# Queueing the modulation products behind the last traced VectorE instruction

## The chip, the cores and the metric

The kernel runs on one core of a Trainium2 chip. The metric is the device time of one execution in microseconds. The program is written in a tile language: a trace of instructions is written out in Python, and a scheduler then fixes the order of each engine's queue at build time, by data dependences, buffers and priorities. On the chip each queue is worked off in that order. The engines are TensorE (PE; its weight loads are PEld), VectorE (DVE), ScalarE (ACT), GpSimd (POOL), and SyncE (SP), which issues the DMAs.

## The reference

Two layers of a diffusion backbone on 256 latent tokens and 256 context tokens, 1024 features wide. A layer is: half-step SwiGLU feed-forward, three token mixers side by side, half-step SwiGLU feed-forward. Each of them is modulated by nine vectors per stream that come from a conditioning vector:

```python
sc, scc = silu(c), silu(c_ctx)
mx = (sc @ w_ada[i] + b_ada[i]).reshape(bsz, N_MOD, 1, D_MODEL)     # latent
mc = (scc @ w_ada[i] + b_ada[i]).reshape(N_MOD, D_MODEL)            # context
def half_ffn(h, g_pre, g_post, shift, scale, gate, w1, w2):
    return 0.5 * gate * rms_norm(swiglu(modulate(rms_norm(h, g_pre), shift, scale), w1, w2), g_post)
```

`w_ada` is 1024 x 9216 per layer: a matrix times two vectors, and large to load. The feed-forward has 2816 hidden features. Shift, scale and gate of the first feed-forward are modulations 0 to 2, of the mixers 3 to 5, of the second feed-forward 6 to 8.

## The kernel before

Activations lie with features on the 128 partitions and 512 tokens (context, then latent) along the columns. To keep float32 accuracy in the fast matmul format, every weight tile and every activation tile is split into a high and a low half. `wload` loads a 512 KB tile `raw` (3 buffers), ScalarE rounds it to `whi`, VectorE subtracts to get `wlo` (2 buffers each). `gemm` then runs three matmuls per tile: weight high with activation high and low, weight low with activation high.

`ffn(l, half)` works in three slabs of hidden features (8, 7 and 7 tiles of 128). A **hidden step** `hidden(k)` projects one pair of tiles: 48 matmuls, then SiLU on ScalarE, the product `gV` on VectorE (line 96), `B` high on ScalarE and `B` low on VectorE (line 102). After a slab's hidden steps come eight **output steps**, which multiply the slab by the output weights and add to `y` (line 99; in slab 0 ScalarE copies). In slab 0 the first `early` steps (4, 5 or 6) run on one 256-column segment at a time, in which norm work of the stage before (`rest`) is woven in; slab 2 also runs one segment after the other; all the rest runs on 512 columns.

The modulation vectors are not matmuls: `ada_block` (line 269) takes one 512 KB tile of `w_ada` (`araw`, 2 buffers, loaded by `ada_fetch` on SP's queue, one block ahead), and multiplies its two halves by the broadcast SiLU of each condition, with a sum along the columns: four VectorE products of 128x512 per block (two where the context is no longer needed, from modulation 5 of layer 1 on), each followed by a read of the accumulator (line 288). After each eighth block small additions finish one vector.

`tick(share)` hands these blocks out in the feed-forward: `due` is the number of blocks that the stage owes (48 in `ffn(0,0)`, 40 in `ffn(0,1)`, 40 in `ffn(1,0)`), and each step earns a share of it: 2 of `whole` after a 512-column hidden step beyond `early`, 1 after an output step of slabs 0 and 1 and after a hidden step of slab 2's first segment, half of one after that segment's output steps. `whole` is 49, 47 and 45. A block is traced under `high_priority(offset=-100)`: the scheduler treats it as if it stood 100 instructions later, so that it fills gaps. That priority is all that orders it against the feed-forward work. The trace is scheduled as a whole, so a block whose tile has landed can also be issued long before the place where it was traced. `cols` (line 372) reads finished vectors and traces at once what is still missing of them (`need`). In layer 0, `vectors()` queues the loads of constants on SP's queue behind the last load of `w_ada`.

Of the kernel before, what the change touches and what calls it, by code (L numbers as in the profile page):

```python
# [58 lines left out]
class Net:  # L59
# [238 lines left out]
    def tick(self, share):  # L298

        self.credit += share * self.due  # L300
        while self.credit > 0.999 and self.todo:
            self.credit -= 1
            with self.tc.high_priority(offset=-100):
                self.ada_block(*self.todo.pop(0))

    def need(self, l, j):
# [1255 lines left out]
```

## Time and profile before

| | us |
|---|---|
| median of 3 runs | 2545.29 |
| lowest and highest | 2538.87, 2552.49 |
| the profiled execution's own time | 2550.41 |
| its span, first to last instruction | 2548.6 |
| PE busy | 2425.2 |
| DVE busy | 1819.8 |
| ACT busy | 1159.9 |
| POOL busy | 289.1 |

The mean granted clock of TensorE is 0.977 of full speed. Busy time of PE includes time at the slow clock, and pipelined matmuls overlap, so a busy PE is not PE at its peak. Products of line 288 by the ticks run from 84 to 284 us, from about 1110 to 1310 and from about 1505 to 1653. The stages can be told by their steps: in `ffn(0,0)` the hidden steps of slab 0 end at 155 us, of slab 1 at 286, and slab 2 runs from 325 to 446, with the first segment's hidden steps up to 363 and its output steps up to 382. In `ffn(0,1)` the first segment of slab 2 runs from 1360 to 1419, in `ffn(1,0)` from 1738 to 1796.

### The profile page before, as it was taken

To read this page: it belongs to the slowest core of one execution; us is meant where nothing else is said; L and a number is where in the kernel's file an instruction comes from. 1 tells how busy PE (TensorE), PEld (TensorE's weight loads), DVE (VectorE), ACT (ScalarE), POOL (GpSimd) and SP (SyncE) were. 2 spreads that over 40 slices of the span, in tenths; PEclk is the share of its full clock that TensorE was granted. 3 is DMA by queue.
4 is the path that set the end of the run, shared out by engine and by line. 5 is a ranking of instruction groups with operands and counts; after the bars stand their busy time and mean duration, and the time that the engine had idled before them with its cause. 6 is when DMAs were issued, how large, how long until landed. Compare 5 with 4: busy or idle time off the path is not lost. (4 is left out here: it accounts for less than half of the span.)

```text
span 2548.6 us, 40627 instructions
## 1 busy us (share of the span) xinstructions
PE 2425.2 (95%) x15554; PEld 2119.7 (83%) x15554; DVE 1819.8 (71%) x3820; ACT 1159.9 (46%) x1935; POOL 289.1 (11%) x288
## 2 busy tenths in 40 slices
PE   6999999999999999989999999999999889998998
PEld 4878799777788767888789998889978779887997
DVE  5898658899875564588864798635789977675555
ACT  3422246656443443563323563224566534455443
POOL 1000002202100111230000230000221110011001
PEclk8999999999999999989999999999999889998999
DMA  6676456443212412556754558735554332433654
GB/s 236 206 223 217 154 176 205 142 149 104 88 53 72 132 53 80 187 164 229 239 167 154 181 184 267 256 100 161 179 174 149 88 101 86 165 127 122 190 185 138
DMA packets 150796, 400.58 MB, mean 157 GB/s; under 512 B 39621, under 2 KB 50629, under 8 KB 150601
## 3 DMA queue, kind: packets, MB, share of 16 engines
q1 hardware_dynamic: 150600, 397.99, 49.4%
q8 instruction: 122, 2.00, 0.3%
q14 instruction: 74, 0.60, 0.1%
HBM read 382.72 MB, written 15.20 MB: 156 GB/s over the span
## 5 line engine op out<-in xcount | busy, mean ns | idle before, releaser
L114 PE MATMUL mm<-B,whi 128*128 128x256 f32 (+1 forms) x7632 | 1325.6, 322 | 35.0 <-ACT B L93 18.0
L114 PEld LDWEIGHTS mm<-B,whi 128*128 128x128 f32 x7632 | 1116.7, 190 | 156.8 <-ACT B L93 21.5
L93 ACT ACTIVATE whi<-raw 128x1024 fp32r<-128x1024 f32 (+1 forms) x506 | 524.6, 1037 | 583.4 <-PE mm L114 537.0
L102 DVE TENSOR_TENSOR wlo<-raw,whi 128x1024 fp32r<-128x1024 f32 (+1 forms) x506 | 613.8, 1214 | 169.9 <-ACT whi L93 141.5
L114 PE MATMUL mm<-B,wlo 128*128 128x256 f32 (+1 forms) x3816 | 692.6, 320 | 10.1 <-DVE wlo L102 10.0
L114 PEld LDWEIGHTS mm<-B,wlo 128*128 128x128 f32 x3816 | 565.6, 188 | 67.5 <-DVE wlo L102 13.9
L114 PE MATMUL mm<-B,araw 128*128 128x512 f32 (+1 forms) x1104 | 224.9, 351 | 4.7 <-DVE araw L102 4.2
L114 PEld LDWEIGHTS mm<-B,araw 128*128 128x128 f32 x1104 | 176.8, 191 | 31.9 <-DVE araw L102 5.6
L288 DVE SCALAR_TENSOR_TENSOR araw<-araw,P 128x512 f32<-128x512 f32 x256 | 167.8, 685 | 28.2 <-DMA araw<-in_w_ada 28.1
L93 ACT ACTIVATE B<-gV 128x256 fp32r<-128x256 f32 (+1 forms) x124 | 58.1, 468 | 241.7 <-DVE gV L96 241.5
L99 POOL TENSOR_TENSOR gm<-gm,ge 128x256 f32<-128x256 f32 x33 | 33.9, 1027 | 1110.0 <-ACT ge L93 1106.0
L288 DVE SCALAR_TENSOR_TENSOR gx<-araw,P 128x512 f32<-128x512 f32 x192 | 125.8, 687 | 41.9 <-DMA araw<-in_w_ada 41.6
L96 DVE TENSOR_TENSOR gV<-gS,mm 128x256 f32<-128x256 f32 (+1 forms) x124 | 59.7, 481 | 108.3 <-PE mm L114 93.4
L99 DVE TENSOR_TENSOR P<-P,mm 128x256 f32<-128x256 f32 (+1 forms) x88 | 43.2, 491 | 103.9 <-PE mm L114 103.9
L105 DVE SCALAR_TENSOR_TENSOR cv<-xp,vec,cv 128x512 f32<-128x512 f32 (+1 forms) x160 | 111.4, 704 | 2.1 <-ACT cv L93 1.4
L93 ACT ACTIVATE gS<-mm 128x256 f32<-128x256 f32 (+1 forms) x172 | 75.4, 439 | 33.9 <-PE mm L114 31.8
L102 DVE TENSOR_TENSOR araw<-raw,araw 128x1024 fp32r<-128x1024 f32 x56 | 70.0, 1250 | 27.2 <-PE mm L114 13.7
L93 ACT ACTIVATE araw<-raw 128x1024 fp32r<-128x1024 f32 x56 | 59.3, 1059 | 60.3 <-PE mm L114 43.0
L99 POOL TENSOR_TENSOR P<-P,gV 128x512 f32<-128x512 f32 (+1 forms) x30 | 36.1, 1203 | 238.9 <-DVE gV L105 235.4
L102 DVE TENSOR_TENSOR B<-gV,B 128x256 fp32r<-128x256 f32 (+1 forms) x124 | 62.4, 503 | 0.0
L93 ACT ACTIVATE B<-gR,mod 128x256 fp32r<-128x256 f32 x88 | 43.3, 501 | 34.7 <-DVE gR L105 25.8
L102 POOL TENSOR_TENSOR B<-gK,B 128x256 fp32r<-128x256 f32 x44 | 43.9, 998 | 111.5 <-ACT gK L93 111.5
(269 smaller groups left out, 2206.6 us busy)
## 6 DMA issues: line engine op xcount, KB each, us to landing
raw<-in_w_ffn_in SPq DMA_DIRECT2D x248, 512.0 KB, 4.1
raw<-in_w_in SPq DMA_DIRECT2D x144, 512.0 KB, 3.6
araw<-in_w_ada SPq DMA_DIRECT2D x130, 512.0 KB, 4.4
raw<-in_w_ffn_out SPq DMA_DIRECT2D x88, 448.0 KB, 3.3
raw<-in_w_ffn_out SPq DMA_DIRECT2D x32, 512.0 KB, 4.5
raw<-in_w_branch SPq DMA_DIRECT2D x24, 512.0 KB, 3.6
raw<-in_w_out SPq DMA_DIRECT2D x24, 512.0 KB, 3.6
P<-keep SPq DMA_DIRECT2D x20, 256.0 KB, 5.9
```

The lines of the kernel that those rows point to most:

```text
L93: self.nc.scalar.activation(out=out, in_=in_, func=func, **kw)
L96: (eng or self.nc.vector).tensor_tensor(out, a, b, op=ALU.mult)
L99: (eng or self.nc.vector).tensor_tensor(out, a, b, op=ALU.add)
L102: (eng or self.nc.vector).tensor_tensor(out, a, b, op=ALU.subtract)
L105: self.nc.vector.scalar_tensor_tensor(out, a, s, b, op0=op0, op1=op1)
L114: self.nc.tensor.matmul(out, lhsT=lhsT, rhs=rhs, start=start, stop=stop)
L288: self.nc.vector.scalar_tensor_tensor(o, wh, 1.0, self.cond[s][h], op0=ALU.mult, op1=ALU.mult, accum_out=c)
```

## The change

In `tick`, the last VectorE instruction traced so far is looked up, and the block is traced under `issue_after` of it: each VectorE instruction of the block gets an edge for the order of issue, behind that instruction on VectorE's queue. It is an edge of order alone, with no wait for a result. The block's DMA on SP is not on VectorE and gets no edge. Blocks traced by `need` are not touched.

```diff
         while self.credit > 0.999 and self.todo:
             self.credit -= 1
-            with self.tc.high_priority(offset=-100):
+            after = next(i for i in reversed(self.nc.cur_bb.bb.instructions) if i.engine == mybir.EngineType.DVE)
+            with self.tc.high_priority(offset=-100), self.tc.issue_after(after):
                 self.ada_block(*self.todo.pop(0))
```

## Rows read from the trace of the kernel before

**Rows 1.** The page's busy times: us, share of the span, instructions.
```profile
PE 2425.2 (95%) x15554; PEld 2119.7 (83%) x15554; DVE 1819.8 (71%) x3820; ACT 1159.9 (46%) x1935; POOL 289.1 (11%) x288
```

**Rows 2.** PE's waits, 80:340 and 1105:1345 (total, times, longest); busy by engine, 1500:1660.
```profile
PE mm L114 <- ACT B L93: 8.2, 2, 4.4
PE mm L114 <- DVE wlo L102: 2.8, 4, 1.0
PE mm L114 <- DVE B L102: 0.6, 1, 0.6
...
PE mm L114 <- ACT B L93: 2.4, 1, 2.4
...
1500.00:1660.00 160.00, 157.40 (x892) 137.16 (x892) 126.88 (x295) 61.06 (x88) 6.30 (x5) 1.00 0.78 253
```

**Rows 3.** Slices of 10 us: PE, PEld, DVE, ACT, POOL busy; PE clock; DMA share, GB/s.
```profile
150.00:160.00 10.00, 5.00 (x15) 3.47 (x15) 9.76 (x32) 2.17 (x3) 0.00 (x0) 0.83 0.65 211
...
170.00:180.00 10.00, 10.00 (x45) 8.23 (x44) 9.06 (x25) 3.03 (x4) 0.00 (x0) 1.00 0.72 226
...
280.00:290.00 10.00, 6.06 (x18) 4.12 (x17) 7.58 (x21) 1.58 (x2) 0.00 (x0) 0.79 0.50 169
290.00:300.00 10.00, 10.00 (x40) 8.07 (x40) 1.74 (x3) 1.91 (x2) 0.00 (x0) 0.87 0.29 93
```

**Rows 4.** Timeline, slab 0's end in `ffn(0,0)`: start, us, what, [idle before, releaser].
```profile
149.83 1.31 PE L114 MATMUL mm<-B,wlo 128*128 128x512 f32 x5
...
154.18 0.68 DVE L96 TENSOR_TENSOR gV<-gS,mm 128x512 f32<-128x512 f32 x1
...
155.58 0.51 PE L114 MATMUL mm<-B,whi 128*128 128x512 f32 x1 [4.44 <-ACT B L93]
```

**Rows 5.** Instructions of line 288 alone: one hidden step, then `ffn(0,0)` from 80.
```profile
142.40:154.20 11.80, 7.58 (x26) 1.00 0.75 236
...
80.00:340.00 260.00, 122.50 (x384) 0.98 0.63 200
```

**Rows 6.** DVE's timeline: two hidden multiplies with no products between.
```profile
1676.00 0.69 DVE L96 TENSOR_TENSOR gV<-gS,mm 128x512 f32<-128x512 f32 x1 [4.28 <-PE mm L114]
...
1686.99 0.69 DVE L96 TENSOR_TENSOR gV<-gS,mm 128x512 f32<-128x512 f32 x1 [4.28 <-PE mm L114]
```

**Rows 7.** Columns of rows 3: slab 2's first segments (hidden, output), then early steps of `ffn(1,0)`.
```profile
325.00:363.00 38.00, 38.00 (x338) 38.00 (x336) 21.46 (x28) 19.47 (x28) 0.00 (x0) 1.00 0.58 184
363.00:382.00 19.00, 19.00 (x164) 19.00 (x163) 12.23 (x20) 10.58 (x16) 3.09 (x3) 1.00 0.64 189
...
1360.00:1399.00 39.00, 39.00 (x333) 39.00 (x332) 20.97 (x28) 19.09 (x27) 0.00 (x0) 1.00 0.58 179
1399.00:1419.00 20.00, 20.00 (x172) 20.00 (x171) 13.17 (x22) 11.28 (x17) 3.15 (x3) 1.00 0.60 187
...
1506.00:1549.00 43.00, 43.00 (x366) 42.94 (x366) 41.81 (x88) 24.47 (x42) 5.59 (x4) 1.00 0.74 237
```

**Rows 8.** Line 288, whole span: what DVE sat idle for (us, times).
```profile
  DMA araw<-in_w_ada: 69.7, 69
```

**Rows 9.** Tile `masks`: first reader (duration ns min/median/max, first and last start).
```profile
L114 PE MATMUL ps<-gV,masks x8: 275/275/310, 493.8 to 1907.8; 128*128 128x48 f32 x8
```

**Rows 10.** Timelines beside and after GpSimd work; GpSimd's group in slab 2's first segment.
```profile
1108.61 1.69 POOL L99 TENSOR_TENSOR gAV<-gAV,ge 128x256 f32<-128x256 f32 x1 [1.46 <-ACT ge L93]
1109.62 0.96 DVE L102 TENSOR_TENSOR B<-gV,B 128x256 fp32r<-128x256 f32 x1
...
1116.68 0.41 DVE L102 TENSOR_TENSOR B<-gV,B 128x256 fp32r<-128x256 f32 x1
...
L99 POOL TENSOR_TENSOR gm<-gm,ge 128x256 f32<-128x256 f32 x3 | 3.1, 1029 | 300.9 <-ACT ge L93 300.9
```

**Rows 11.** SP's queue, 80:340: waits of `ada_fetch` for its buffer (total, times, longest).
```profile
SPq L266 <- DVE araw L288: 70.0, 40, 3.1
```

## The prediction

> **What bounds the kernel now.** I read the busy shares first. TensorE (PE) is busy 95% of 2548.6 us [rows 1], so an edit that only reorders VectorE (DVE) work can win back no more than PE's idle time and its slow-clock time, and only in the stretches that the edit touches. The products of `ada_block` (line 288) are issued by ticks in three feed-forward stages: `ffn(0,0)`, `ffn(0,1)` and `ffn(1,0)`. So the second view is PE's waits in those three stretches [rows 2]. In the first, PE waits 8.2 us in two waits for ScalarE's high half of a hidden tile (`B`), 2.8 us for a weight low half and 0.6 us for a hidden low half: 11.6 us. In the second, one such wait of 2.4 us. In the third PE idles 160.0 - 157.4 = 2.6 us in all.
>
> The reader is to see in [rows 3] what such a wait costs beyond itself. At the full clock 10 us hold 45 matmuls. The slice 150 to 160 has 5.00 us of PE time but only 15 matmuls (22.5 would fit), at a granted clock of 0.83; 280 to 290 has 18 in 6.06 us (27 would fit), at 0.79; 290 to 300 has 40. The missing 7.5, 9 and 5 at 10/45 = 0.22 us are 4.8 us lost to the lower of the clock's two levels after the two long waits. In the other two stretches the clock stays at 1.00.
>
> Who is late? [rows 4] shows the chain at the end of the first slab. PE has its last matmul of hidden step 7 done at 149.83 + 1.31 = 151.14. The DVE multiply that makes the hidden tile (`gV`, line 96) runs only at 154.18, and PE resumes at 155.58, through ScalarE. In between DVE was working off products: between two such multiplies (142.4 to 154.2) there are 26 instructions of line 288, that is 13 products, each with its accumulator read [rows 5]. The ticks trace less than that: 48 blocks over 49 shares, two shares a step, are 1.96 blocks, and at four products a block 7.8 products a step. So products traced after this step's multiply already stand in front of it. They were free to: nothing but their own data tied them to a place. An undisturbed 512-column step takes 10.99 us [rows 6]; the disturbed one took 11.8.
>
> **The change part by part.** No computation or DMA is added or removed. Each block's DVE instructions must be issued behind the last DVE instruction traced before its tick: after a hidden step that is the low half of that step's own tile (or a later step of the woven norm work), in an output step the weight's low half or the accumulation.
>
> *The slab ends.* The step of [rows 5] had 11.8 us of DVE, of which 13 products at 122.50/192 = 0.64 us are 8.3 us; 3.5 us are other work. With eight products it is 8 x 0.64 + 3.5 = 8.6 us against PE's 10.99, so the multiply is no longer late: five products fewer are 3.2 us, against a lateness of 3.04. Gone then, at most: 11.6 + 4.8 + 2.4 + 2.6 = 21.4 us. At least: if order within the step still leaves the multiplies half as late, about 11. I take 21.4, since eight products leave 2.4 us spare.
>
> *The waits for the products' own weights.* DVE stood 69.7 us in 69 waits at the head of its queue for `araw` to land [rows 8]. With two buffers and at most two blocks a step these loads get a step's time, and much of this goes. I count it at nothing by itself: what it cost PE is in the 21.4.
>
> *Where the products go.* They can no longer run ahead, so the last ones land in slab 2's first segment, where today there is none. For `ffn(0,0)` that is 7 hidden steps of 0.98 block and 8 output steps of 0.49, or 10.8 blocks of 4 x 0.64 = 2.55 us: 27.5 us of DVE. The segment has 38 + 19 = 57 us, PE has no gap in it, and DVE is busy 21.5 + 12.2 us [rows 7]. The sum is 61.2, so 4.2 us too much. For `ffn(0,1)` (40 blocks over 47 shares) it is 9.4 blocks or 23.9 us, on 21.0 + 13.2, which makes 58.1 of 59 us: full. For `ffn(1,0)` (40 over 45) it is 9.8 blocks, by then of two products each, 12.5 us: room enough. Cover: the blocks are traced with a priority 100 instructions later than their place, so overflow can slip into the second segment. Low end of this cost: 0 (below nothing is excluded, PE has no idle time there). High end: the 4.2 us fall on PE, and both full segments end with a wait like the 4.44 us of [rows 4] and its 1.7 us of slow clock: 4.2 + 12.3 = 16.5 us. I take 4, nearer the low end, because a row carries a like load: 1506 to 1549 of `ffn(1,0)`, also 256-column steps, has 41.8 of 43 us of DVE, 237 GB/s, and PE busy throughout [rows 7].
>
> *What moves with it on SP's queue.* The loads of `araw` follow their buffers, about 90 us later at the end of `ffn(0,0)`; the constants that `vectors()` queues behind the last of them (masks, rotary tables) come as much later. The masks are first read at 493.8 us [rows 9] and the last tick's block runs near 385, so nothing is late. `cols` asks for modulation 4 at the end of slab 1, when 37 of 48 blocks are traced and 24 are needed.
>
> *A rule against it.* Beside a GpSimd operation the 128x256 low half took 0.96 us, without one 0.41 [rows 10]. The Trainium skill ("SBUF — State Buffer", section "Who interferes with whom") says that a VectorE instruction with two SBUF inputs and a GpSimd instruction that reads SBUF exclude one another for a whole instruction. The trace agrees in kind. Products have two SBUF inputs and would now stand beside GpSimd's three sums of squares in each segment [rows 10]. By the rule in full, 3 x 1.03 us in each of the two full segments, the cost would be 6.2 us and the forecast 2 us later. By the row it is 3 x 0.55 us in each, 3.3 us, which lies inside the 4.
>
> **Sum.** 21.4 - 4 = 17.4 us off the profiled execution's 2550.4, which gives 2533. The runs' median, 2545.3, is 5.1 lower, and the same difference gives 2528. The runs span 13.7 us (0.54%), so half a per cent (12.7 us) is about what can be told from no change.
>
> **The rivals.**
> *Slab 2 takes it back.* The cost is its high end, 16.5: net 5, 2540. For it: DVE at 61.2 of 57 us. Against: the second segment and the priority as cover. Chance 0.22.
> *Slower: SP's queue becomes the bound.* A load of `araw` waits on SP for its buffer, with the weight loads queued behind it: 70.0 us in 40 waits, 1.75 each [rows 11]. In 512-column steps a weight tile is due every 5.3 us (24 matmuls at 0.22) and hides that; in slab 2 every 2.7 us (24 at 38/338). If DVE lags and the 10.8 + 9.4 + 9.8 = 30 loads that move there each pass the wait on to PE: 52.5 us, less 21.4, so +31 and 2576. It decides once the wait exceeds what the third `raw` buffer covers (about one tile, 2.7 us; the longest wait so far is 3.1). Against: 1506 to 1549 loads at 237 GB/s in such steps without a PE gap. Chance 0.12.
> *The change does little.* The scheduler already placed most blocks behind their step, or other late work keeps the waits: 2545. Against: 13 products where 7.8 are traced, and none at all in slab 2. Chance 0.12.
> The forecast, 2528 with a range of its own from 2519 to 2539: chance 0.54.
>
> **How the numbers follow.** Faster by over 0.5% is below 2532.6: about 0.7 of the forecast's chance and a fifth of the first rival's, 0.42. Slower by over 0.5% is above 2558: the second rival and little else, 0.13. The rest, 0.45, is within. The range reaches down to 2514 (no cost in slab 2, and a run at the low end of the spread) and up to 2556 (both mild rivals with the spread); it leaves out the slower rival.
>
> **What would show it.** Right: no wait of PE over 1 us at the ends of slabs 0 and 1 of `ffn(0,0)`, no slice below 0.95 there, seven to nine products between two hidden multiplies, none before the fifth hidden step, products in the slab 2 segments until about 385 us, and the 69.7 us of DVE waits for `araw` below 30. Wrong: new PE waits for `wlo` or `B` in slab 2, or SP's waits for `araw` above 2.7 us there.

## The result and the profile after

The changed kernel takes 2512.1 us (median of 5 runs, 2511.01 to 2519.57), the kernel before 2544.3 (5 runs on the same chip, 2538.87 to 2552.49). The ratio is 0.9878, with a 95% interval of 0.9864 to 0.9893: 32 us faster by the medians. Measured a second time, on another occasion (`c_after_again` below), it was 2517.16 against 2544.13, ratio 0.9891 (0.9867 to 0.9916): 27 us. The forecast of 2528 was too high: the first median lies 1.9 us under the range (2514 to 2556), the second inside it.

The busy times of the changed kernel answer to [rows 1]. Its span is 2509.2 us, its mean granted clock 0.984 where it was 0.977.

```profile
PE 2404.5 (96%) x15554; PEld 2107.3 (84%) x15554; DVE 1819.5 (73%) x3820; ACT 1165.7 (46%) x1935; POOL 289.7 (12%) x288
```

PE lost 20.7 us of busy time with the same 15,554 matmuls; DVE's busy time is as it was. So part of what went was no wait but matmuls at the lower clock.

PE runs its matmuls in the same order in every kernel of this study, but for at most 190 of 15,554 places (4 between before and after). The stages can therefore be cut at matmuls of the same number, and compared one by one, without regard to when they run. All times are us from one profiled execution each, PE's idle time in brackets where there was any that matters.

| stage | before | before again | after | after again |
|---|---|---|---|---|
| `ffn(0,0)`, slabs 0 and 1 after the early steps | 221.4 (11.8) | 219.4 (11.7) | 202.9 (0.0) | 202.9 (0.0) |
| its slab 2 | 119.5 | 119.5 | 119.7 | 120.9 (1.0) |
| mixers, layer 0 | 595.7 | 597.9 | 594.5 | 596.4 |
| `ffn(0,1)`, slabs 0 and 1 | 197.4 (4.6) | 199.1 (4.8) | 191.9 (0.0) | 191.9 (0.0) |
| its slab 2 | 126.7 | 126.7 | 126.4 (0.7) | 127.5 (0.3) |
| `ffn(1,0)`, slabs 0 and 1 | 184.8 (2.6) | 186.2 (2.8) | 181.1 (0.0) | 181.1 (0.0) |
| its slab 2 | 121.0 | 121.0 | 119.5 | 121.0 |
| mixers, layer 1 | 446.8 | 442.5 | 438.5 | 439.5 |

By the means of two traces each, slabs 0 and 1 of the three stages gained 17.5 + 6.3 + 4.4 = 28.2 us, and the three slabs 2 together lost 0.3 (367.2 before; 365.6 and 369.4 after). That is 27.9 us, and it lies between the two measured differences. Layer 1's mixers, where no tick hands out a product, are 5.7 us shorter by the same means; what is known of that stands in the last section.

The reader is to see first that the stalls and their aftermath are gone. These are the 10-us slices that answer to [rows 3], with the same columns: 45 or 46 matmuls in each, at full clock.

```profile
150.00:160.00 10.00, 10.00 (x46) 8.19 (x45) 9.27 (x29) 3.21 (x4) 0.00 (x0) 1.00 0.66 222
...
170.00:180.00 10.00, 10.00 (x45) 8.19 (x45) 9.49 (x27) 3.32 (x4) 0.00 (x0) 1.00 0.82 252
...
280.00:290.00 10.00, 10.00 (x45) 8.20 (x44) 9.26 (x27) 2.08 (x3) 0.00 (x0) 1.00 0.74 236
290.00:300.00 10.00, 10.00 (x45) 8.22 (x44) 9.73 (x28) 2.02 (x2) 0.00 (x0) 1.00 0.71 224
```

The timelines of DVE and of PE at the end of slab 0 answer to [rows 4]. The multiply `gV` now waits for PE (2.53 us idle before it), it no longer keeps PE waiting: it starts at 145.62, and PE goes from the weight low half of one tile to the next without a bracket of idle time.

```profile
145.62 0.69 DVE L96 TENSOR_TENSOR gV<-gS,mm 128x512 f32<-128x512 f32 x1 [2.53 <-PE mm L114]
146.22 1.22 DVE L102 TENSOR_TENSOR wlo<-raw,whi 128x1024 fp32r<-128x1024 f32 x1
147.36 0.68 DVE L102 TENSOR_TENSOR B<-gV,B 128x512 fp32r<-128x512 f32 x1
147.96 0.69 DVE L288 SCALAR_TENSOR_TENSOR gx<-araw,P 128x512 f32<-128x512 f32 x1
```

```profile
148.55 1.77 PE L114 MATMUL mm<-B,wlo 128*128 128x512 f32 x7
150.15 0.62 PE L114 MATMUL mm<-B,whi 128*128 128x512 f32 x2
150.61 0.39 PE L114 MATMUL mm<-B,wlo 128*128 128x512 f32 x1
150.84 2.45 PE L114 MATMUL mm<-B,whi 128*128 128x512 f32 x10
```

Line 288 alone, in the hidden step before that, answers to [rows 5]: 16 instructions, eight products, where the prediction counted 13. Below it is what DVE sat idle for on that line in the whole run, against 69.7 us in [rows 8].

```profile
134.60:145.60 11.00, 5.06 (x16) 1.00 0.59 193
```

```profile
  DMA araw<-in_w_ada: 6.1, 12
```

The first segment of slab 2 answers to [rows 7]: hidden steps, output steps, and then the beginning of the second segment, all engines. After it, the same three stretches with line 288 alone on DVE.

```profile
304.00:342.00 38.00, 38.00 (x334) 37.88 (x333) 37.30 (x86) 18.43 (x27) 0.00 (x0) 1.00 0.86 274
342.00:361.00 19.00, 19.00 (x162) 18.82 (x162) 19.00 (x43) 9.90 (x15) 2.02 (x2) 1.00 0.82 269
361.00:400.00 39.00, 39.00 (x332) 38.95 (x331) 36.83 (x79) 21.41 (x36) 10.06 (x9) 1.00 0.77 237
```

```profile
304.00:342.00 38.00, 17.30 (x55) 1.00 0.86 274
342.00:361.00 19.00, 9.71 (x26) 1.00 0.82 269
361.00:400.00 39.00, 5.90 (x18) 1.00 0.77 237
```

DVE is busy 56.3 of 57 us there, and PE has no gap. The eighteen instructions of line 288 in the third stretch (nine products) are the overflow. SP's waits for a buffer of `araw`, 300 to 400, answer to [rows 11]: 7.1 us in 6 waits, and the longest, 2.0, stays under the 2.7 us that the third `raw` buffer was to cover.

```profile
SPq L266 <- DVE araw L288: 7.1, 6, 2.0
```

### The profile page after: what moved, and what is told of

The parts are those of the page before. It is cut to its first block, busy times and chain, and to the rows that moved or that the text cites. A ratio compares the mean times of both kernels' runs of the same rounds, so it can differ in the third digit from the quotient of the medians.

```text
span 2509.2 us, 40628 instructions
## 1 busy us (share of the span) xinstructions
PE 2404.5 (96%) x15554; PEld 2107.3 (84%) x15554; DVE 1819.5 (73%) x3820; ACT 1165.7 (46%) x1935; POOL 289.7 (12%) x288
## 5 line engine op out<-in xcount | busy, mean ns | idle before, releaser
L99 POOL TENSOR_TENSOR P<-P,gV 128x512 f32<-128x512 f32 (+1 forms) x30 | 37.2, 1239 | 237.2 <-DVE gV L105 233.7
```

The source lines that it names most:

```text
L99: (eng or self.nc.vector).tensor_tensor(out, a, b, op=ALU.add)
```

## The experiments

Each is an edit of the changed kernel, unless the text says that it is one of the kernel before. Ratios are against the kernel before on the same chip, with the 95% interval.

**The kernel before once more.** No edit.

> The kernel before, unchanged, for a second trace. In the first pair of traces the second layer's mixers (from the last accumulation of ffn(1,0) to the output projection) were 8.4 us shorter after the change, with no product in them and PE's waits alike. Theory A, spread of the clock between executions: ratio 1.000 within 0.002, and this stretch comes out 3 us or more shorter than in the first trace of before (447 us). Theory B, the stretch is slower in this kernel than in the changed one: again 446 to 448 us.

Measured: 2546.45 us, ratio 0.9998 (0.9983 to 1.0013); its stages are in the table. PE idles 11.7, 4.8 and 2.8 us in the three stages where it was 11.8, 4.6 and 2.6: the stalls come back with the same order of the queues. Layer 1's mixers moved by 4.4 us with no edit.

**The edge in the first stage alone, and in the other two alone.**

```diff
-            with self.tc.high_priority(offset=-100), self.tc.issue_after(after):
+            with self.tc.high_priority(offset=-100), (
+                    self.tc.issue_after(after) if self.due == 48 else nullcontext()):
```

> Order edge in ffn(0,0) alone. Theory A, the gain is made stage by stage where products stood in front of the hidden multiply, and adds up: 18 to 20 us below the kernel before, about 2525. Theory B, the gain is mostly made elsewhere (second layer, mixers): under 10 us.

The second kernel has `!= 48`.

> Order edge in ffn(0,1) and ffn(1,0) alone. Theory A (the stages add up): 8 to 12 us below the kernel before, about 2534, and with the run of ffn(0,0) alone the full gain of 28 to 34. My prediction's sizes for these two stages (2.4 and 2.6) would give 5 us.

Measured: the first stage alone 2525.56, ratio 0.9917 (0.99 to 0.9933), 21 us; the other two alone 2535.99, ratio 0.9957 (0.994 to 0.9974), 11 us. Together that is the whole 32, each with an interval of some 4 us to either side. Slabs 0 and 1 follow the edge: with it in the first stage they take 202.9, and `ffn(0,1)` and `ffn(1,0)` take 198.8 and 183.8, near what they took before; with it in the others, 221.6, then 191.9 and 181.1. PE's waits of the second kernel from 80 to 303 are those of [rows 2] again:

```profile
PE mm L114 <- ACT B L93: 8.6, 2, 4.6
PE mm L114 <- DVE wlo L102: 2.1, 2, 1.3
PE mm L114 <- DVE B L102: 0.7, 2, 0.6
```

So the stages don't depend on one another, and the later two are worth 11 us where the prediction had 5.

**Products of one column instead of 512**, with the edge and, in the kernel before, without it.

```diff
-                wh = w[:, h * T:(h + 1) * T]
+                wh = w[:, h * T:h * T + 1]
...
-                o = wh if s == conds[-1] else self.t("gx", [P, T], 2)
+                o = wh if s == conds[-1] else self.t("gx", [P, T], 2)[:, :1]
```

> The changed kernel with each product cut from 512 columns to one (the modulation vectors are then other numbers); loads, order and count of instructions stay. Theory A, after the change the products are hidden everywhere, slab 2 included: within 3 us of the changed kernel, 2509 to 2513. Theory B, as predicted, VectorE is full in slab 2's first segment and it costs 4 us or more: 2500 to 2508.

> The kernel before (no order edge), each product cut from 512 columns to one (other modulation values). Loads stay, and with them VectorE's waits at the head of its queue for tiles that have not landed. Theory A, it is the products' own time in front of the hidden multiply that costs: nearly all of the 28 us in the three stages goes (slabs 0 and 1 of ffn(0,0) at 203 to 207 us instead of 221). Theory B, it is the waits for landing: most of it stays (over 212 us), with over 50 us of VectorE waits for araw.

Measured: with the edge 2517.43, ratio 0.9888 (0.9869 to 0.9907). Products that take 0.16 us instead of 0.69 make the changed kernel no faster: its slabs 0 and 1 are at 202.9, 191.9 and 181.1 with either. What the products cost PE in them is therefore nothing after the change. Without the edge 2520.94, ratio 0.9905 (0.9887 to 0.9924); slabs 0 and 1 of the first stage at 202.9, with PE idle 0.0, and those of `ffn(0,1)` at 194.9, also without idle time (the matmuls there stand 233 ns apart instead of 229; see the last section). Yet DVE stood waiting for `araw` longer than in any other kernel:

```profile
its engine sat idle before it (us, times) until:
  DMA araw<-in_w_ada: 168.2, 114
```

So products that run ahead and wait for their tiles cost PE nothing in the first stage, as long as they are short. What made the multiply late was the products' own time in front of it, not the waits for the tiles.

**The edge on the block's load in place of its products.** The last instruction looked up is SP's, so that the load is held behind it in SP's queue and the products are free.

```diff
-            after = next(... if i.engine == mybir.EngineType.DVE)
+            after = next(... if i.engine == mybir.EngineType.SP)
```

> The order edge put on the block's load (behind the last DMA traced) instead of on its products. A product can then be ahead of its place only as far as its load is. Theory A, place is what counts: part of the gain, 10 to 25 us, as run-ahead shrinks to about the one block loaded ahead. Theory B, waits for landing count: products still follow each landing at once, so little gain, 0 to 8 us.

Measured: 2528.71, ratio 0.9934 (0.991 to 0.9958). Slabs 0 and 1 are at 202.9, 191.9 and 181.7: a product can then be ahead of its place only as far as its load is, so either end does it there. But slab 2 takes 124.6 (PE idle 1.5) and 128.2 (idle 2.2), with the waits where the first segment's hidden steps end. Which order makes that cost was not followed up.

**No offset of priority.**

```diff
-            with self.tc.high_priority(offset=-100), self.tc.issue_after(after):
+            with self.tc.issue_after(after):
```

> The changed kernel without the priority offset of 100: products stand right at their traced place, ahead of weight halves traced later. Theory A, the edge alone makes the gain: within 3 us of the changed kernel. Theory B, the offset is what covers slab 2: PE waits for weight halves there, 4 to 15 us slower.

Measured: 2528.12, ratio 0.9933 (0.9915 to 0.9951). Slabs 0 and 1 at the floor, slab 2 at 124.7 (idle 2.0) and 130.4 (idle 2.4): 5.2 and 3.7 us longer than before the change. The waits of PE from 303 to 434 are for what DVE and ScalarE make for the running step:

```profile
PE mm L114 <- ACT whi L93: 0.9, 1, 0.9
PE mm L114 <- DVE B L102: 0.5, 1, 0.5
PE mm L114 <- DVE wlo L102: 0.4, 1, 0.4
```

The edge is a lower bound for a product's place; the offset is what lets it slip behind the next weight halves. In slab 2, where DVE is full, both are needed.

**No shares for slab 2, first attempt.** The edit takes slab 2's 11 shares out of `whole`, but its ticks stayed, so every share grew by 49/38, and the blocks asked for went beyond the stage's own 48.

```diff
-        whole = 2 * (15 - early) + 16 + (11 if len(segs) == 2 else 0)
+        whole = 2 * (15 - early) + 16
```

> The changed kernel with all blocks handed out in slabs 0 and 1 (2.5 blocks a hidden step, 10 products, by rows 10 x 0.64 + 3.5 = 9.9 of 10.99 us) and none in slab 2. Theory A, products cost nothing as long as a step's sum fits: within 3 us of the changed kernel. Theory B, at 90% of the step the multiplies are late again: 4 to 12 us slower than the changed kernel. If slab 2 had the price I predicted: 4 us faster.

Measured: 2534.72, ratio 0.9962 (0.9946 to 0.9978). It doesn't tell the theories apart as it was meant to, since slab 2 of the first stage got more products, 66 instead of 48. It shows another thing: slabs 0 and 1 stay at 202.9 with 8 or 12 products a hidden step, while slab 2 of the first stage takes 137.6, with PE idle 12.1 (303 to 434):

```profile
PE mm L114 <- ACT whi L93: 8.1, 6, 1.9
PE mm L114 <- DVE wlo L102: 4.0, 3, 2.3
```

That slab's cost of 18.1 us shows that the price of the first rival, 16.5 us over two stages, can come due: DVE is full there, and the changed kernel has no room for many more products.

**No shares for slab 2, second attempt**, with the ticks taken out too, and the changed kernel once more.

```diff
-        whole = 2 * (15 - early) + 16 + (11 if len(segs) == 2 else 0)
+        whole = 2 * (15 - early) + 16
...
-                    elif a == 0:
-                        self.tick(1 / whole)
...
-                        if a == 0:
-                            self.tick(0.5 / whole)
```

> The changed kernel with no share handed out in slab 2: all 48 (40, 40) blocks of a stage are earned in slabs 0 and 1, 2.53 blocks (10.1 products) a 512-column hidden step of the first feed-forward instead of 1.96. DVE then has 10.1 x 0.64 + 3.5 = 10.0 us in such a step against PE's 10.99. Theory (products behind the multiply cost nothing as long as a step's DVE work is below PE's step, and slab 2 costs nothing in the changed kernel): slabs 0 and 1 stay within 0.5 us of 202.9 and 191.9 us, slab 2 of the first feed-forward stays at 119.5, no product in slab 2 but a block or two that slips over its start, and the time is that of the changed kernel, 2507 to 2522. Rival (slab 2's share is needed, a step has room for eight products only): new waits of PE for B or the weight's low half at the ends of slabs 0 and 1, those two stretches 5 us or more longer, 2522 to 2535.

> The changed kernel once more, for the spread of one trace. Theory (the gain stands in the three feed-forward stages, and what the mixers differ by is the clock of the single execution): slabs 0 and 1 at 202.9 and 191.9 us and the third stage at 181.1 to within 0.3 us, PE idle 0.1 us or less in the first two; the mixers' stretches of both layers within 4 us of either earlier trace, up or down. Rival (the change also gains in the mixers): layer 1's mixers again at 438 to 439 us against 442 to 447 before. Time 2508 to 2520, ratio to the kernel before 0.986 to 0.990.

Measured: 2522.28, ratio 0.9915 (0.9889 to 0.994). The theory holds for slabs 0 and 1 (202.9, 191.9, 181.1, PE idle 0.0), though the steps take 8 and 12 products in turn and DVE has no gap in those of 12. It fails at slab 2's start, which it put at 119.5 and which took 126.4. The last blocks reach over into steps of half the length, and there stand in front of the multiply and of the weight's low half. DVE's timeline shows a product that waits for its tile, three more, then the multiply and the low half; PE's shows who waited:

```profile
318.19 0.69 DVE L288 SCALAR_TENSOR_TENSOR gx<-araw,P 128x512 f32<-128x512 f32 x1 [1.41 <-DMA araw<-in_w_ada]
...
320.73 0.41 DVE L96 TENSOR_TENSOR gV<-gS,mm 128x256 f32<-128x256 f32 x1
...
321.21 1.22 DVE L102 TENSOR_TENSOR wlo<-raw,whi 128x1024 fp32r<-128x1024 f32 x1
```

```profile
322.49 2.08 PE L114 MATMUL mm<-B,wlo 128*128 128x256 f32 x8 [3.78 <-DVE wlo L102]
```

```profile
320.00:330.00 10.00, 7.51 (x51) 7.52 (x52) 7.09 (x19) 4.20 (x7) 0.00 (x0) 0.83 0.54 164
```

A wait of 3.78 us and then a granted clock of 0.83 (part of the slice at 1.2 GHz, the lower of the clock's two levels, the rest at 2.4) make some 5.6 of the 6.9 us between them: the stall of [rows 3 and 4], moved. The rest is the slower of two paces at which the matmuls behind it run (last section). Slab 2's shares are worth having, for this reason and not because a 512-column step has no room.

The second trace of the changed kernel has the same floors to 0.1 us. Its time and ratio lie where both theories put them. Layer 1's mixers came out short again, at 439.5, half a microsecond beyond the 438 to 439 that the rival had named; this run doesn't refute the rival.

No version beat the changed kernel: the thin products, which leave work out, came closest.

## Why the prediction was wrong, step by step

The mechanism held, and two terms of the sum failed: what `ffn(0,1)` had to gain, which was put too low, and what slab 2 would cost, which was put too high.

*The slab ends of the first stage* were put at 11.6 of waits and 4.8 of slow clock, 16.4 us. Measured: 17.5. The mechanism was right in its detail: eight products between multiplies (four in the first step that has any), 10.99 us a step, no product before the fifth hidden step (the first at 115.0), no wait of PE from 80 to 340, no slice below full clock. One count was off: between the multiplies of 142.35 and 154.18 the timeline before has twelve products, not 13 (the other two instructions in the window of [rows 5] are the ends of neighbours at its edges), and 0.68 us of waits for tiles. Twelve are still far more than the 7.8 that were traced for a step.

*The same in `ffn(0,1)`* was put at 2.4 and measured 6.3 (5.5 and 7.2 by trace). This is the step of the sum that was most off. The view of PE's waits of [rows 2] has two more lines for that stage, which the sum left out:

```profile
PE mm L114 <- ACT whi L93: 1.7, 1, 1.7
PE mm L114 <- DVE B L102: 0.6, 1, 0.6
```

With the 2.4 that is 4.7, the idle time that went. The wait of 0.6 comes right behind the one of 2.4, at the same slab end. The wait of 1.7 ends some 52 us later, and there ScalarE is late: its timeline before the change shows 10.42 us without work, at the head of its queue an instruction that waits for a load, and behind it the weight's high half.

```profile
1252.63 0.63 ACT L93 ACTIVATE P<-P 128x512 f32<-128x512 f32 x1 [10.42 <-DMA P<-in_cb]
1253.16 1.04 ACT L93 ACTIVATE whi<-raw 128x1024 fp32r<-128x1024 f32 x1
```

After the change ScalarE waits for that load nowhere in the stage: the loads of `in_cb` go out on SP at 1213.6 to 1220, when before they went out one by one from 1247.3 to 1256.1, between loads of `araw` and of weights. ScalarE has no such wait with the edge in the two later stages alone, and waits up to 6.9 us for such a load with the edge in the first stage alone. The edge changed when loads are issued, not only when products run.

Beside the idle time 0.8 us went by the first trace of before and 2.4 by the second. In the first, which the forecast was made from, the clock stays at 1.00, as the prediction says; the 0.8 are some 0.27 us around each of the three waits, in which PE counts as busy but its matmuls stand further apart. In the second trace 1.6 of the 2.4 are the lower clock: behind the last wait sixteen matmuls take 5.51 us, at a granted clock of 0.83 from 1250 to 1260. Before and before again:

```profile
1254.26 3.94 PE L114 MATMUL mm<-B,whi 128*128 128x512 f32 x16 [1.70 <-ACT whi L93]
```

```profile
1253.82 5.51 PE L114 MATMUL mm<-B,whi 128*128 128x512 f32 x16 [1.82 <-ACT whi L93]
```

*`ffn(1,0)`* was put at 2.6, its idle time, and measured 4.4 (3.7 and 5.1 by trace): the idle time was right, and PE's time around the waits was missing, 1.1 us at full clock in the first trace and 2.4 in the second, where the granted clock is 0.83 from 1577 to 1587. The window that answers to the last of [rows 2], 1500 to 1660, has no idle time left:

```profile
1500.00:1660.00 160.00, 160.00 (x809) 135.95 (x808) 88.42 (x177) 53.94 (x68) 0.00 (x0) 1.00 0.55 174
```

*Slab 2* was put at a cost of 4, between 0 and 16.5, and measured 0.3 over all three stages. Some of that is luck: the matmuls of a first segment run at one of two paces, 1.6 us apart over the segment (last section). The second trace after the change has the paces of both traces before, and its slabs 2 are 2.2 us longer than theirs; the first has the fast pace in two slabs where they have the slow one, and is 1.6 longer with that allowed for. At equal pace slab 2 thus cost some 2 us. The load was foreseen well: 81 instructions of line 288 in the first segment (one counts in both windows) are 40 products, where 10.8 blocks of four had been worked out, and DVE stands at 56.3 of 57 us. What failed is the choice within the bounds. The overflow of 4.2 us hardly fell on PE; it moved into the second segment, nine products of it, and the run without the offset shows by what: there slab 2 cost 5.2 us. The sign of being wrong that the prediction named, new waits of PE for `wlo` or `B` in slab 2, did come in the second trace, at 0.2 and 0.8 us.

*The rule against it* was met in kind. Two products of that segment stand beside GpSimd's sums of squares and take 1.24 and 1.23 us; the first of them by the timelines of GpSimd and DVE:

```profile
352.25 1.00 POOL L99 TENSOR_TENSOR gm<-gm,ge 128x256 f32<-128x256 f32 x1 [274.54 <-ACT ge L93]
```

```profile
352.57 1.24 DVE L288 SCALAR_TENSOR_TENSOR araw<-araw,P 128x512 f32<-128x512 f32 x1
```

The product ends 0.56 us after GpSimd's instruction (353.81 and 353.25), and takes 0.55 longer than the 0.69 of the others: the row's price. The Trainium skill ("SBUF — State Buffer", section "Who interferes with whom") has the two contend through the read interface that they share, an exclusive lock. The trace agrees that they don't overlap freely; the product began 0.32 us behind GpSimd's instruction and lost 0.55, less than the 0.68 that was left of it and not the full 1.03 of the prediction's larger price. PE did not wait for it.

*The waits for `araw`* fell from 69.7 to 6.1 (below 30 was expected), and were worth nothing by themselves, as counted: the thin products without the edge waited 168.2 us and kept the first stage's floor.

*The rivals.* Slab 2 takes it back: no, by 0.3 against 16.5 us, though 66 products there instead of 48 made it so (18.1 us in the first stage alone). SP's queue: no, in none of the three slabs 2 did a wait for a buffer of `araw` last over 2.0 us. It does little: no.

In sum, 17.5 + 6.3 + 4.4 - 0.3 = 27.9 stands against 16.4 + 2.4 + 2.6 - 4 = 17.4. Of the 10.5 us between them 3.9 are the second stage, 3.7 slab 2 (of which 1.6 are the pace), 1.8 the third stage and 1.1 the first. The first measurement, 32.2, holds 4.3 us more, which lie outside these stages and for which no cause is shown; the second, 27.0, holds 0.9 less. The range's low end took the full 21.4 as the most that could go; the waits that the profile showed and the sum left out made that bound too tight.

## What to carry to other kernels

When queues are ordered at build time by data alone, background work on an engine runs ahead and stands in front of the one late operation that paces another engine; an edge of order behind that operation costs nothing and takes the whole stall away, if the work fits into the step's slack. Add up all of the bound engine's idle time in the stretch, and its time around each wait (here 0.27 us or more, and in some executions slow-clock time as well), whatever engine the wait is put down to: late work shows up under several names. Where the engine has no slack left, let the work slip further back as well, and keep it out of the first short step.

## What the runs showed that had not been expected

**Two paces of the same matmuls.** In the first segment of slab 2 the 256-column matmuls follow one another in one of two rhythms, though instructions, order and operands are the same. These windows of 34 us in the three slabs 2, before and then after, touch 302 or 303 matmuls (one every 113.3 ns) or 291 (117.8 ns), at full clock both.

```profile
326.00:360.00 34.00, 34.00 (x302) 34.00 (x302) 19.22 (x25) 17.90 (x26) 0.00 (x0) 1.00 0.58 185
1361.00:1395.00 34.00, 34.00 (x291) 34.00 (x290) 18.70 (x24) 16.89 (x25) 0.00 (x0) 1.00 0.59 183
1738.00:1772.00 34.00, 34.00 (x291) 34.00 (x290) 18.64 (x25) 16.86 (x24) 0.00 (x0) 1.00 0.58 182
```

```profile
306.00:340.00 34.00, 34.00 (x302) 34.00 (x301) 33.84 (x78) 17.53 (x25) 0.00 (x0) 1.00 0.86 277
1334.00:1368.00 34.00, 34.00 (x302) 34.00 (x301) 31.98 (x74) 17.62 (x25) 0.00 (x0) 1.00 0.82 271
1709.00:1743.00 34.00, 34.00 (x303) 34.00 (x302) 26.02 (x51) 17.88 (x26) 0.00 (x0) 1.00 0.83 261
```

A pace holds for a whole run of hidden steps and is worth 1.6 us over 354 matmuls: the 121.0 and 119.5 of `ffn(1,0)`'s slab 2. A busy DVE does not bring the slow one, and the changed kernel shows both. The 512-column matmuls have a second pace too: 233 ns instead of 229 in most of `ffn(0,1)` with thin products and no edge, which is all of its 3.0 us over the floor. What sets the pace is open.

**The clock in the mixers.** One stretch of layer 1's mixers, 500 matmuls with no idle time of PE and no product, takes 37.2 us or about 33 to 34. The rows are of before, before again and after:

```profile
2060.00:2098.00 38.00, 38.00 (x504) 32.60 (x503) 26.91 (x56) 14.18 (x27) 1.93 (x3) 0.86 0.24 76
```

```profile
2061.00:2095.00 34.00, 34.00 (x501) 29.43 (x500) 25.88 (x54) 14.38 (x27) 2.18 (x3) 0.96 0.30 88
```

```profile
2028.00:2062.00 34.00, 34.00 (x502) 29.38 (x501) 26.24 (x56) 13.94 (x27) 1.88 (x2) 0.96 0.28 82
```

The granted clock makes the difference, 0.86 against 0.96 (more or less of the stretch at 1.2 GHz instead of 2.4), and the kernel before shows both. The seven traces of kernels that have an edge in all three stages all show the short form, and four of the five others the long one. Layer 1's mixers as a whole take 438.5 to 441.8 us in the seven and 442.5 to 446.8 in the five. So in these traces a gain of some microseconds goes with the edge; by what way, and whether it would hold in more traces, is not shown.
